# A hybrid decoder layer on one core: the input scales of all token tiles worked out beside the first pair's

## The chip, the cores and the metric

The kernel runs on one core of one Trainium2 chip. The metric is the device time of one execution in microseconds. The core has five engines with instruction queues of their own, each worked off in order: PE (matrix products and transposes), DVE (vector work), ACT (elementwise functions), POOL (here mainly indirect loads and additions) and SP (which issues transfers). They wait for each other by semaphores.

## The reference

One decoder layer over x of 1024 tokens by 1024 features, f32, depth 1:

```
h  = x
xn = rmsnorm(h, norm_mix)                       # x * rsqrt(mean(x*x) + 1e-6) * gain
z  = xn @ w_in ; q, k, v, a, gt = split(z)
attn = dilated causal attention(rope(q), rope(k), v), 8 heads of 64,
       patterns (128,1), (512,4), (2048,16) merged by their softmax denominators
c    = silu(layernorm(depthwise causal conv of 31 taps(a * sigmoid(gt)) + conv_b))
h += concat(rmsnorm(attn), rmsnorm(c)) @ w_out
xn = rmsnorm(h, norm_ffn)
s  = (xn @ peer_wq) against two tables of 128 sub-keys, 8 heads;
     top 16 of each half, top 16 of their sums -> 128 experts of 16384 per token, softmax gate
h += sum_k gelu(xn . expert_u[e_k]) * gate_k * expert_v[e_k]
h += sigmoid(rmsnorm(h, norm_ple) @ w_ple_gate) * (p @ w_ple_proj)
out = rmsnorm(h, final_norm)
```

The change concerns the first line's mean of squares of x alone.

## The kernel before, in words

The 1024 tokens are eight tiles of 128, taken in four pairs (GROUPS). A pair g goes through stages: stage_in (normed_input, then qkv), stage_attend (attend, then convolve), stage_out (mixed, project, normed_ffn), stage_search and stage_combine. They are written in the order in0, attend0, then for pair 0 out0, search0, in1, combine0, attend1, then in2, out1, search1, attend2, combine1, then in3, out2, search2, attend3, combine2, and last out3, search3, combine3. "Pair 1" below means tiles 2 and 3, the second pair.

normed_input is what the change splits. It takes the pair's two tiles xt (tag "xn", two buffers, loaded by SP), squares each on ACT with a running sum (sqj_mix, L146), takes the root on ACT (sd_mix, L151) and the reciprocal on DVE (r_mix, L153), scales xt by it on ACT (L286), transposes each xt in two batches of four through one PSUM bank (pt_mix, L162) and evicts each batch to xT with the gain (ACT, L167). PE's products for k, q, v (L261) and for the convolution's a and gt (L270) read xT.

Three PSUM banks with the tag "lin" serve k, q, v, a, gt, the output products, and the sums cs of the convolution as well. convolve works out 13 of the 31 taps as ACT products (tap, L349) that POOL adds into side (L350), with three tap buffers, and 18 taps as a chain on DVE in a lin bank (L353, L356); cc (L358) adds both and frees the bank. mixed transposes cc on PE (pc, L423) for the layer norm.

Retrieval is done in two ways. Tiles 2 to 5 (ALL) go through a dense product with every expert (dense): 128 steps of key columns, PE's longest part. Tiles 0, 1, 6, 7 (FEW) fetch their 128 rows of expert_u and of expert_v per token by indirect loads, 1024 transfers that POOL issues (L596), with one multiply-and-sum on DVE each (L609 for u, L625 for v) and a ring of six buffers. embed is the last stage: the dense tiles and tile 0 first, then tiles 1, 6 and 7.

The order of each engine's instructions is fixed when the kernel is built: a scheduler walks through the written program and, by its own estimate of when operands are ready, puts the ready instruction of the highest priority next. Stages that are written one behind the other so run interleaved, and the gathers, which have the lowest priority, fill what the scheduler holds to be gaps on DVE. On the chip the queues then run in that order, whatever is ready.

## Time and profile before

| | us |
|---|---|
| median of three runs | 3139.38 |
| the three runs | 3140.76, 3117.92, 3139.38 |
| profiled execution | 3130.95 |
| its span, from the first to the last instruction | 3129.1 |
| mean granted clock of TensorE, of full speed | 0.943 |
| first matmul of the dense product starts | 1412.15 |

Read the table with the sections of the program in mind: up to 1412 us come the four pairs and the making of the dense product's gates, then the dense product to about 2928, then the last embeds. Queries of the trace give busy time by stretch, the waits of an engine with what released it, and the single instructions in order of time. In these, "idle before" is the time in which the engine did nothing before the instruction, and the arrow names what came last of what it waited for.

### The profile page before, as it was taken

What the parts mean: (1) busy time and instruction counts of PE and PEld (TensorE: products, weight loads), DVE (VectorE), ACT (ScalarE), POOL (GpSimd) and SP (SyncE); (2) the same over time, 40 slices, a digit from 0 to 9 for tenths busy, and PEclk for the clock granted to TensorE, in tenths of its full rate; (3) what the DMA queues carried; (4) which work ended last, traced back from release to release, by engine and by line L of the source; (5) the groups of instructions that cost most, each with busy time, mean ns of one, the idle gap of its engine ahead of it and who ended that gap; (6) DMA issues with size and microseconds to landing.
All of it is one profiled execution on the core that took longest, in us unless ns stands there. A gap on an engine that the chain in (4) does not pass through costs nothing. (4 is left out here: it accounts for less than half of the span.)

```text
span 3129.1 us, 36005 instructions
## 1 busy us (share of the span) xinstructions
PE 2734.5 (87%) x11711; PEld 2003.1 (64%) x11711; DVE 2503.7 (80%) x5164; ACT 1133.9 (36%) x2084; POOL 1495.5 (48%) x1220
## 2 busy tenths in 40 slices
PE   6588948977995689968999999999999999999986
PEld 3465624853674376647777777777777777777643
DVE  1528877998797889977898888988888888888871
ACT  2523443274244329963222222222222222222342
POOL 0400676454436430134655655666655656655640
PEclk9799978988998799989999999999999999999998
DMA  4154859846854775799999999999999999998970
GB/s 166 54 175 140 311 203 361 302 149 233 319 202 161 266 272 154 231 297 333 346 351 331 340 326 352 350 350 351 339 331 332 347 340 344 339 334 321 332 261 24
DMA packets 304527, 865.75 MB, mean 277 GB/s; under 512 B 26779, under 2 KB 93747, under 8 KB 304339
## 3 DMA queue, kind: packets, MB, share of 16 engines
q0 software_dynamic: 147456, 536.94, 47.3%
q1 hardware_dynamic: 153616, 323.16, 29.8%
q10 hardware_dynamic: 3266, 3.36, 0.3%
q8 instruction: 92, 1.51, 0.2%
q14 instruction: 97, 0.79, 0.1%
HBM read 819.83 MB, written 43.52 MB: 276 GB/s over the span
## 5 line engine op out<-in xcount | busy, mean ns | idle before, releaser
L596 POOL DMA_INDIRECT u<-in_expert_u_dram,ex x512 | 675.9, 1320 | 822.3 <-DVE hk L609 547.1
L596 POOL DMA_INDIRECT v<-in_expert_v_dram,ex x512 | 671.5, 1312 | 510.7 <-DVE gy L625 376.9
L625 DVE SCALAR_TENSOR_TENSOR gy<-v,ga,gy 128x1024 f32<-128x1024 f32 x512 | 657.8, 1285 | 41.0 <-DMA v<-in_expert_v_dram,ex 31.9
L609 DVE CUSTOM_DVE_ANT_0 u<-u,gxn 128x1024 f32<-128x1024 f32 x512 | 613.7, 1226 | 54.5 <-DMA u<-in_expert_u_dram,ex 53.4
L741 PE MATMUL ph<-xh,uh 128*128 128x512 f32 x1024 | 407.4, 398 | 43.5 <-DMA gt<-gate_d 29.0
L743 PE MATMUL ph<-xh,ul 128*128 128x512 f32 x1024 | 409.5, 400 | 21.5 <-DVE ul L719 21.1
L759 ACT CAST vh<-v 128x1024 fp32r<-128x1024 f32 x128 | 131.5, 1051 | 757.1 <-PE kept_y L774 516.2
L742 PE MATMUL ph<-xl,uh 128*128 128x512 f32 x1024 | 404.9, 395 | 0.0
L741 PEld LDWEIGHTS ph<-xh,uh 128*128 128x128 f32 x1024 | 196.2, 192 | 91.2 <-ACT uh L717 49.0
L743 PEld LDWEIGHTS ph<-xh,ul 128*128 128x128 f32 x1024 | 195.4, 191 | 75.9 <-DVE ul L719 35.4
L761 DVE TENSOR_TENSOR vl<-v,vh 128x1024 fp32r<-128x1024 f32 x128 | 154.2, 1225 | 109.7 <-ACT vh L759 109.2
L350 POOL TENSOR_TENSOR side<-side,tap 128x256 f32<-128x256 f32 x192 | 147.8, 772 | 193.8 <-ACT tap L349 132.4
L772 PE MATMUL py<-vh,ah 128*128 128x512 f32 x512 | 204.8, 400 | 38.4 <-ACT ah L751 38.4
L270 PE MATMUL pq<-x2T,w_pq 128*128 128x256 f32 x1024 | 231.4, 384 | 4.8 <-DMA w_pq<-in_peer_wq_dram 3.4
L742 PEld LDWEIGHTS ph<-xl,uh 128*128 128x128 f32 x1024 | 196.2, 192 | 41.9
L270 PEld LDWEIGHTS pq<-x2T,w_pq 128*128 128x128 f32 x1024 | 194.2, 193 | 34.0 <-issue 3.4
L773 PE MATMUL py<-vl,ah 128*128 128x512 f32 x512 | 201.7, 397 | 0.0
L774 PE MATMUL kept_y<-vh,al 128*128 128x512 f32 x512 | 199.7, 390 | 0.0
L772 PE MATMUL kept_y<-vh,ah 128*128 128x512 f32 x512 | 199.5, 390 | 0.0
L774 PE MATMUL py<-vh,al 128*128 128x512 f32 x512 | 199.2, 397 | 0.3 <-DVE al L753 0.3
L773 PE MATMUL kept_y<-vl,ah 128*128 128x512 f32 x512 | 199.4, 389 | 0.0
L717 ACT CAST uh<-u 128x1024 fp32r<-128x1024 f32 x128 | 134.2, 1048 | 108.8 <-DMA u<-in_uT_dram 67.7
(264 smaller groups left out, 4683.0 us busy)
## 6 DMA issues: line engine op xcount, KB each, us to landing
u<-in_uT_dram SPq DMA_DIRECT2D x128, 512.0 KB, 6.9
v<-in_expert_v_dram SPq DMA_DIRECT2D x128, 512.0 KB, 6.3
w_pq<-in_peer_wq_dram SPq DMA_DIRECT2D x64, 512.0 KB, 5.0
gate_d<-stage SPq DMA_DIRECT2D x16, 2048.0 KB, 11.8
gt<-gate_d SPq DMA_DIRECT2D x64, 512.0 KB, 10.1
w_o<-in_w_out_dram SPq DMA_DIRECT2D x32, 512.0 KB, 4.8
w_k<-in_w_qkv_dram SPq DMA_DIRECT2D x16, 512.0 KB, 6.3
w_q<-in_w_qkv_dram SPq DMA_DIRECT2D x16, 512.0 KB, 4.4
```

Source lines behind the costliest of these rows:

```text
L270: nc.tensor.matmul(a, w[:, k, :], xT[:, k, :], start=k == 0, stop=k == KD - 1)
L350: G.tensor_tensor(side, side, m, ALU.add)
L596: d = G.indirect_dma_start(out=e, out_offset=None, in_=table, in_offset=bass.IndirectOffsetOnAxis(ap=index, axis=0))
L609: uses(V.tensor_tensor_reduce(out=e, in0=e, in1=xn, scale=1.0, scalar=0.0, op0=ALU.mult, op1=ALU.add, accum_out=hk[:, k : k + 1]))
L625: uses(V.scalar_tensor_tensor(y, e, act[:, k : k + 1], y, ALU.mult, ALU.add))
L741: nc.tensor.matmul(ph, hi, xh[:, k, :], start=k == 0, stop=False)
L742: nc.tensor.matmul(ph, hi, xl[:, k, :], start=False, stop=False)
L743: nc.tensor.matmul(ph, lo, xh[:, k, :], start=False, stop=k == KD - 1)
L761: V.tensor_tensor(b, v, a.bitcast(F32), ALU.subtract)
L772: nc.tensor.matmul(py, ah[e][:, rows(j)], vh[e][:, half(f)], start=first, stop=False)
L773: nc.tensor.matmul(py, ah[e][:, rows(j)], vl[e][:, half(f)], start=False, stop=False)
L774: nc.tensor.matmul(py, al[e][:, rows(j)], vh[e][:, half(f)], start=False, stop=last_e)
```

## The change

The mean of squares is taken out of normed_input. input_scales(g, xs) works out r for a pair and keeps its columns in r_mix; pair 0's is called just ahead of stage_in(0). later_scales, called behind stage_in(0), loads the six tiles of pairs 1 to 3 a second time (xq2 to xq7, tag "t4", two buffers, on SP's queue) and works out their scales. normed_input then only scales and transposes. The reciprocals get a tag of their own ("r_mix", four buffers).

```diff
--- before.py
+++ after.py
@@ -138,18 +138,18 @@
     acc = bank(ps_keep, "acc", 1)
 
 
-    def rstd(srcs, n, name, junk=None, pool=small):
+    def rstd(srcs, n, name, junk=None, pool=small, r_tag="r"):
 
         ssq = pool.tile([P, len(srcs)], F32, tag="ssq", name=f"ssq_{name}", bufs=2)
         for j, src in enumerate(srcs):
             sq = junk(f"sqj_{name}_{j}") if junk else mpool.tile([P, D], BF16, tag="t2", name=f"sqj_{name}_{j}", bufs=3)
             S.activation(sq[:, :n], src, AF.Square, accum_out=ssq[:, j : j + 1])
-        return inv_sqrt(ssq, 1.0 / n, name, pool)
-
-    def inv_sqrt(v, scale, name, pool=small):
+        return inv_sqrt(ssq, 1.0 / n, name, pool, r_tag)
+
+    def inv_sqrt(v, scale, name, pool=small, r_tag="r"):
         sd = pool.tile([P, v.shape[1]], F32, tag="sd", name=f"sd_{name}", bufs=2)
         S.activation(sd, v, AF.Sqrt, bias=eps, scale=scale)
-        r = pool.tile([P, v.shape[1]], F32, tag="r", name=f"r_{name}", bufs=4)
+        r = pool.tile([P, v.shape[1]], F32, tag=r_tag, name=f"r_{name}", bufs=4)
         V.reciprocal(r, sd)
         return r
 
@@ -279,11 +279,24 @@
             xs.append(xt)
         return xs
 
+    def input_scales(g, xs):
+        r = rstd(xs, D, f"mix{g}", r_tag="r_mix")
+        for j, i in enumerate(GROUPS[g]):
+            r_mix[i] = r[:, j : j + 1]
+
+    def later_scales():
+        for g in range(1, NG):
+            xs = []
+            for i in GROUPS[g]:
+                xt = mpool.tile([P, D], F32, tag="t4", name=f"xq{i}", bufs=2)
+                nc.sync.dma_start(xt, x_d[rows(i), :])
+                xs.append(xt)
+            input_scales(g, xs)
+
     def normed_input(g, xs):
-        r = rstd(xs, D, f"mix{g}")
         xT = apool.tile([P, KD, GN], F32, tag="xT", name=f"xT{g}")[:, :, : len(xs) * P]
         for j in range(len(xs)):
-            S.activation(xs[j], xs[j], AF.Copy, scale=r[:, j : j + 1])
+            S.activation(xs[j], xs[j], AF.Copy, scale=r_mix[GROUPS[g][j]])
             transpose_to(xT[:, :, rows(j)], xs[j], KD, f"mix{g}_{j}", tps, g_mix)
         return xT
 
@@ -826,7 +839,7 @@
     xs = load(0)
     load_tables()
     fetched, wide, h1s = {}, {}, {}
-    st = {}
+    st, r_mix = {}, {}
 
     def stage_in(g):
         xT = normed_input(g, xs if g == 0 else load(g))
@@ -854,7 +867,9 @@
             else:
                 wide[i] = combine(i, vals[j], idxs[j], mpool, ND)
 
+    input_scales(0, xs)
     stage_in(0)
+    later_scales()
     stage_attend(0)
     for g in range(NG - 1):
         if g > 0:
```

The kernel's lines behind the new function are 13 further down in the changed file, those of the last part 15.

The first place is the opening on ACT. sqj_mix is a Square with its sum, xt and xq are tiles of x, sd_mix a root, skT the copy of the transposed sub-keys:

```order
 L146 ACTIVATE sqj_mix_1_164,ssq_mix_161<-xt_105 128x1024
+L146 ACTIVATE sqj_mix_0_367,ssq_mix_366<-xq_362 128x1024
+L164 COPY skT<-pt_sk_157 128x256
 L151 ACT_TABLE_LOAD
 L151 ACTIVATE sd_mix_166<-ssq_mix_161,eps 128x2
-L164 COPY skT<-pt_sk_157 128x256
-L286 ACTIVATE xt_103<-xt_103,r_mix_168 128x1024
-L286 ACTIVATE xt_105<-xt_105,r_mix_168 128x1024
+L146 ACTIVATE sqj_mix_1_369,ssq_mix_366<-xq_364 128x1024
+L299 ACTIVATE xt_103<-xt_103,r_mix_168 128x1024
+L299 ACTIVATE xt_105<-xt_105,r_mix_168 128x1024
+L151 ACTIVATE sd_mix_371<-ssq_mix_366,eps 128x2
```

The root of pair 0 and the table load ahead of it have moved behind skT, and Squares and roots of the later pairs stand between them and the scaling of pair 0's tiles.

The second place is PE at the input of pair 2 (tiles 4 and 5), behind the last convolution product a_3. Before:

```order
L270 MATMUL a_3_2290<-xT_1545,w_a_3_2288 128x256 x8
L162 MATMUL pt_mix_0_0_2554<-cst,xt_2539 128x128 x4
L261 MATMUL k_0_2592<-w_k_0_2594,xT_2552 128x512
L162 MATMUL pt_mix_0_4_2563<-cst,xt_2539 128x128 x4
L261 MATMUL k_0_2592<-w_k_0_2594,xT_2552 128x512
L261 MATMUL k_0_2592<-w_k_1_2600,xT_2552 128x512
L162 MATMUL pt_mix_1_0_2573<-cst,xt_2541 128x128 x4
L261 MATMUL k_0_2592<-w_k_1_2600,xT_2552 128x512
L261 MATMUL k_1_2593<-w_k_0_2594,xT_2552 128x512
L162 MATMUL pt_mix_1_4_2582<-cst,xt_2541 128x128 x4
```

and with the change:

```order
L270 MATMUL a_3_2320<-xT_1575,w_a_3_2318 128x256 x8
L162 MATMUL pt_mix_0_0_2575<-cst,xt_2569 128x128 x4
L162 MATMUL pt_mix_0_4_2584<-cst,xt_2569 128x128 x4
L162 MATMUL pt_mix_1_0_2594<-cst,xt_2571 128x128 x4
L162 MATMUL pt_mix_1_4_2603<-cst,xt_2571 128x128 x4
L261 MATMUL k_0_2613<-w_k_0_2615,xT_2573 128x512 x2
L261 MATMUL k_0_2613<-w_k_1_2621,xT_2573 128x512 x2
L261 MATMUL k_0_2613<-w_k_2_2627,xT_2573 128x512 x2
L261 MATMUL k_1_2614<-w_k_0_2615,xT_2573 128x512 x2
L261 MATMUL k_1_2614<-w_k_1_2621,xT_2573 128x512 x2
```

The four batches of transposes used to alternate with matmuls of k; now all four stand directly behind a_3, and k's first six matmuls belong to the pair's first tile alone.

The third place is DVE where the dense product begins. ul is the first instruction of it, u_56 is the gather of tile 1's 57th row with its reduction, hk its result. Before:

```order
L609 ISA u_55_19701,hk_19533<-u_55_19701,gxn_19534 128x1024
L609 ISA hk_19533 128x1
L609 ISA u_56_19704,hk_19533<-u_56_19704,gxn_19534 128x1024
L609 ISA hk_19533 128x1
L719 TENSOR_TENSOR ul_9124<-u_9120,uh_9122 128x1024
L609 ISA u_57_19707,hk_19533<-u_57_19707,gxn_19534 128x1024
```

and with the change:

```order
L622 ISA u_35_19653,hk_19545<-u_35_19653,gxn_19546 128x1024
L622 ISA hk_19545 128x1
L622 ISA u_36_19656,hk_19545<-u_36_19656,gxn_19546 128x1024
L622 ISA hk_19545 128x1
L732 TENSOR_TENSOR ul_9136<-u_9132,uh_9134 128x1024
L622 ISA u_37_19659,hk_19545<-u_37_19659,gxn_19546 128x1024
```

Up to this place tile 1 has 57 of its u rows behind it before, and 37 with the change.

## Rows read from the trace of the kernel before

**Rows 1.** Page part 1: busy us (share of span), instructions of each engine.

```profile
PE 2734.5 (87%) x11711; PEld 2003.1 (64%) x11711; DVE 2503.7 (80%) x5164; ACT 1133.9 (36%) x2084; POOL 1495.5 (48%) x1220
```

**Rows 2.** Windows: length; PE, PEld, DVE, ACT, POOL busy; clock; DMA share; GB/s.

```profile
250.00:1412.00 1162.00, 944.57 (x4384) 634.60 (x4382) 986.68 (x2961) 563.25 (x1195) 506.39 (x463) 0.90 0.70 241
1412.00:2928.00 1516.00, 1441.12 (x6148) 1162.92 (x6149) 1326.38 (x1753) 406.92 (x525) 889.38 (x650) 0.98 0.93 339
```

**Rows 3.** Waits of PE, 250 to 1412 us: total, times, longest.

```profile
PE pt_mix L162 <- ACT xt L286: 80.7, 3, 39.3
PE pc L423 <- DVE cc L358: 30.7, 3, 13.8
```

**Rows 4.** Timeline, ACT, opening: start, us, engine, line, operation [idle before].

```profile
17.34 1.06 ACT L146 ACTIVATE sqj_mix<-xt 128x1024 bf16<-128x1024 f32 x1
...
19.54 1.28 ACT L151 ACT_TABLE_LOAD   x1
20.84 0.29 ACT L151 ACTIVATE sd_mix<-ssq_mix,eps 128x2 f32<-128x2 f32 x1
24.39 0.37 ACT L164 COPY skT<-pt_sk 128x256 f32<-128x256 f32 x1 [3.26 <-PE pt_sk L162]
```

**Rows 5.** Timeline, PE, opening: the long run of K.

```profile
34.97 9.61 PE L261 MATMUL k<-w_k,xT 128*128 128x512 f32 x22
```

**Rows 6.** Windows, opening, between the first loads and the next.

```profile
23.00:37.00 14.00, 11.34 (x33) 6.06 (x34) 0.00 (x0) 7.02 (x19) 0.00 (x0) 1.00 0.01 1
```

**Rows 7.** DMA issues of the first 60 us: count, KB, us to landing.

```profile
xt<-in_x_dram SPq DMA_DIRECT2D x2, 512.0 KB, 5.4
```

**Rows 8.** Timeline, pair 1: last score matmul, r_mix, first transposes.

```profile
263.78 0.94 PE L486 MATMUL psc<-skT,pqT 128*128 128x128 f32 x7
...
272.91 0.14 DVE L153 RECIPROCAL r_mix<-sd_mix 128x2 f32<-128x2 f32 x1
...
274.28 1.12 PE L162 MATMUL pt_mix<-cst,xt 128*128 128x128 f32 x4 [9.56 <-ACT xt L286]
```

**Rows 9.** Timeline, pair 2: convolution sums and r_mix on DVE; PE.

```profile
406.53 0.41 DVE L358 TENSOR_TENSOR cc<-cs,side 128x256 f32<-128x256 f32 x1
...
407.76 13.40 DVE L356 SCALAR_TENSOR_TENSOR cs<-glu,cw,cs 128x256 f32<-128x256 f32 x34
421.07 0.41 DVE L358 TENSOR_TENSOR cc<-cs,side 128x256 f32<-128x256 f32 x1
428.13 0.42 DVE L358 TENSOR_TENSOR cc<-cs,side 128x256 f32<-128x256 f32 x1 [6.64 <-POOL side L350]
428.47 0.16 DVE L153 RECIPROCAL r_mix<-sd_mix 128x2 f32<-128x2 f32 x1
...
429.87 1.12 PE L162 MATMUL pt_mix<-cst,xt 128*128 128x128 f32 x4 [39.27 <-ACT xt L286]
...
451.47 1.88 PE L261 MATMUL q<-w_q,xT 128*128 128x512 f32 x4
```

**Rows 10.** Windows, pair 2, behind the convolution.

```profile
440.00:460.00 20.00, 18.46 (x52) 8.53 (x51) 13.04 (x31) 3.38 (x8) 13.27 (x11) 1.00 0.99 385
```

**Rows 11.** Timeline, pair 3: DVE's wait for POOL, and PE.

```profile
713.15 0.42 DVE L358 TENSOR_TENSOR cc<-cs,side 128x256 f32<-128x256 f32 x1 [4.75 <-POOL side L350]
...
716.02 1.12 PE L162 MATMUL pt_mix<-cst,xt 128*128 128x128 f32 x4 [31.88 <-ACT xt L286]
```

**Rows 12.** Lines, DVE, 250 to 1412 us: one v gather's multiply-add.

```profile
L625 DVE SCALAR_TENSOR_TENSOR gy<-v,ga,gy 128x1024 f32<-128x1024 f32 x128 | 165.5, 1293 | 15.0 <-DMA v<-in_expert_v_dram,ex 13.2
```

**Rows 13.** Waits of ACT, 355 to 430 us; windows, attention of pair 1.

```profile
ACT tap L349 <- POOL side L350: 24.3, 44, 2.3
...
300.00:390.00 90.00, 87.82 (x393) 57.46 (x393) 74.03 (x159) 39.32 (x76) 58.21 (x48) 1.00 0.88 305
```

**Rows 14.** Timeline, DVE, tail: last gathers, last embed's start.

```profile
3024.08 5.24 DVE L625 SCALAR_TENSOR_TENSOR gy<-v,ga,gy 128x1024 f32<-128x1024 f32 x4
...
3097.22 0.16 DVE L153 RECIPROCAL r_ple<-sd_ple 128x1 f32<-128x1 f32 x1 [1.00 <-ACT sd_ple L151]
```

## The prediction

> **What bounds the kernel now.** I read the page's totals first: PE is busy for 87% of the span and DVE for 80% [rows 1]. A share over the whole span decides nothing, so next come the stretches [rows 2]. The middle one, the dense product, keeps PE busy for 1441.12 of 1516 us, and the change touches nothing in it. The first 1412 us hold the change. From 250 us to there PE is busy 944.57 of 1162 us. The waits of PE in that stretch say what holds it [rows 3]: 80.7 us in three waits of the input transposes pt_mix for the scaled tile xt, and 30.7 us of pc for the convolution sums cc. Those three waits are what the change aims at, one per later pair. Tracing each back is the next view. For pair 1, PE stands 9.56 us, and the scale 1/rms (r_mix) that xt needs is one row of DVE that runs at 272.91, behind the top-16 search [rows 8]. For pair 2, PE stands 39.27 us. On DVE r_mix is at 428.47, behind 34 convolution steps and a cc that itself waited 6.64 us for POOL [rows 9]. For pair 3 it is 31.88 us, behind a cc that waited 4.75 us [rows 11]. So in each of the three places a 0.16 us reciprocal waits in DVE's order, and PE with it.
>
> **The change, part by part.** Squares, roots, reciprocals, scales and transposes are as many as before, so their cost is a matter of place; new are six loads of 512 KB.
>
> *Opening.* Before, the table load (1.28 us) and the root ran while ACT anyway waited 3.26 us for pt_sk [rows 4]. Now skT's copy stands ahead of the table load, so the load is exposed, with one root (0.29) and the Square of xq3 (1.06 us [rows 4]) before the first xt scale: 1.28 + 0.29 + 1.06 = 2.6 us later. The other Squares stand between the four evictions of xT, where the first scale and eviction leave ACT time between transposes; I add 0.7 us, two thirds of one Square, for what doesn't fit. Sum **+3.3 us** on the long run of K, which began at 34.97 [rows 5]. Bounds: 1.28 + 0.29 = +1.6 if the Squares all fit, and 6 x 1.06 + 1.6 = +8 if none does. The loads themselves cost nothing in bandwidth: the DMA engines were 0.01 busy between 23 and 37 us [rows 6], the landing of such a load took 5.4 us [rows 7], and six times 0.5 MB fill that stretch. If the stretch were full, each would cost its share of the landing, inside the +8.
>
> The rule that speaks against this stands in the Trainium skill, DMA: Bandwidth & Descriptors, section "Anatomy of one DMA": a wait for a semaphore is taken on the issuing sequencer before the transfer is dispatched. By that rule w_k_3 stands on SP's queue behind xq6 and xq7, which wait for buffers that Squares on ACT free, and the opening would come to its upper bound, +8. No row of before has a load blocked in this way, so it shows neither for nor against.
>
> *Pair 1.* The transposes no longer wait for DVE. The last score matmul of the search ends at 264.72, that is 263.78 + 0.94, and pt_mix began at 274.28 [rows 8]: 8.9 us can go, after 0.66 us for the copy that frees its PSUM bank. But ACT now scales pair 2's first tile ahead of pair 1's last eviction, and that tile's load can start only when pair 1's first buffer is read; against the landing of 5.4 us [rows 7] I charge 2 us, since K's first matmuls need only the earlier evictions. **-7 us**, bounds -3 (all 5.4 us shown) and -9. What is late next is DVE, which is busy here.
>
> *Pair 2.* The four transposes now run directly behind a_3, in the gap. The 39.27 us don't go whole, since K still needs PSUM banks in which convolution sums lie: three "lin" banks serve both. K's first tile gets the bank that a cc at 406.53 frees, its second the one of the cc at 421.07 [rows 9]. From there eight matmuls of K on the second tile, and its last weights once a slot is free, take some 10 us: K ends at about 431 instead of 451.47, where q begins [rows 9], which is 20 us for PE. DVE and the gathers don't follow all of it. Behind the convolution come rotary steps and gathers at 1.29 us [rows 12], with the DMA engines at 0.99 from 440 to 460 [rows 10]; in the new order 26 gathers instead of 32 stand from the convolution to the layer norm, and six at 1.29 are 7.7 us; the 6.64 us wait for POOL goes as well, because the side taps start earlier. 7.7 + 6.6 = 14.3, and with the rotary steps no longer waiting for a late K **-15 us**. Bounds: -10 (K starts when the bank is free, at 421.5, and then takes as long as before from its first transpose on, 451.47 - 429.87 = 21.6 us: 443.1, or 8.4 sooner, and the first batch of transposes, 1.12 us, is no longer in it: about 10) and -20.
>
> *Pair 3.* The same with 31.88 us. The wait of 4.75 us for POOL goes and the transposes with their evictions are out of K's way; DVE is full with the combine step up to its layer norm, so I take **-12 us**, pair 2's in the ratio of the two gaps (31.88/39.27 x 15 = 12.2). Bounds -8 and -18.
>
> *Dense and tail.* The gathers fill DVE's idle time, and in the new order tile 1's u rows up to 36 stand ahead of the dense part instead of up to 56: 20 fewer, while the dense part holds as many as before. So about 19 come later, in the tail, at 1.31 us each (5.24 / 4 [rows 14]): 25 us of DVE. The last gather of before ends at 3029.3 (3024.08 + 5.24) and its tile's embed starts only at 3097.2 [rows 14]: 68 us of cover. They stand in DVE's order between the steps of the embeds, so I charge **+4 us**, bounds 0 and +8 (a third of the 25). Without that cover they would cost all 25.
>
> Sum: 3.3 - 7 - 15 - 12 + 4 = -26.7 us. Bounds together: 1.6 - 9 - 20 - 18 + 0 = -45 and 8 - 3 - 10 - 8 + 8 = -5. The profiled execution took 3130.95 us, so **3104 us**; that lies 35 us under the median of the three runs (3139.38), which is itself 8.4 above the profiled one.
>
> The table loads carry a second rule: the Trainium skill, ScalarE: Activation LUTs, section "What ACT_TABLE_LOAD costs", gives about 1.28 us for the load and as much again (1.38) for a drain. Here the root starts 1.30 us after its load [rows 4], so the trace shows no drain; by the skill the opening term would be +4.7.
>
> **The rivals.** A measurement of this kernel can tell about 1% from no change, some 31 us, so 3108 is the upper edge of "faster".
>
> *A, the forecast*: 3086 to 3115, chance 0.48, about two thirds of it under 3108.
>
> *B, given back*: PE is let go early, but the convolution and DVE's order hold the next step. For it: cc already holds PE for 30.7 us [rows 3], and in pair 2's gap DVE runs 34 convolution steps, 13.40 us, in one go [rows 9]. Against: 11.4 us of DVE's own waits for POOL (6.64 + 4.75) stand in the gaps. Terms at their small ends but the opening and tail as taken: 3.3 - 3 - 10 - 8 + 4 = -13.7, or 3117. Chance 0.22, and in it the case that the change does nothing since scales stay behind DVE, which the new order speaks against.
>
> *C, larger*: with the convolution begun earlier, the wait pc on cc goes too. For it: it has 30.7 us and follows the same stage. Half of it, 15, on top of the low bounds -9, -20, -18 with 3.3 + 0: 3130.95 - 59 = 3072. Chance 0.18; a part of it, with less of pc, lies above 3076.
>
> *D, slower*: ACT's order blocks. The scaled input lets the convolution of pair 1 start during its attention, so side taps on ACT now stand between exps, and each tap's buffer comes free by an add on POOL that stands behind a gather. There are 20 gathers between the adds of pair 1 now, 10 before, and 16 in pair 2. The longest such wait was 2.3 us and the sum around pair 1 24.3 us [rows 13], at a time when no exp stood behind. At 2.3 us, 20 of them are 46 us, and with pair 2's 83: 3130.95 - 27 + 46 = 3150, or 3187. Against: ACT is busy only 39.32 of 90 us and PE 87.82 in the stretch with attention [rows 13], so there are 51 us to swallow them. It decides once more than 27 us of the 83 show. Chance 0.12, half of it over 1%.
>
> **The numbers.** Faster by over 1%: two thirds of A and all of C, 0.32 + 0.18 = 0.50. Slower by over 1%: 0.06. Within: 0.16 + 0.22 + 0.06 = 0.44. The range that leaves out 2 in 10 goes from 3076 (leaves about 0.08, in C) to 3134 (leaves about 0.11, in D); A's own is 3086 to 3115.
>
> **What would show it.** The wait of pt_mix for xt should fall from 80.7 us to under 10; the long run of K should begin at about 38 us; pair 2's q should begin near 428 (451.47, less 20, less pair 1's 7, plus 3), the first dense matmul some 31 us earlier than now, and the dense stretch keep its 1516 us. The last gather should end 15 to 30 us nearer to the last embed. Wrong it would be if PE's gap after a_3 has a new releaser of the same length (B), if ACT's taps wait for POOL by far over 24 us with exps behind them (D), or if K's run begins at 42 us or later.

## The result, and the profile after

The changed kernel takes 3120.3 us (median of 20 runs, 3103.04 to 3128.67), the kernel before 3135.2 us beside it (20 runs, 3117.92 to 3144.91): a ratio of 0.995 [0.9936, 0.9963], or 15 us. It is faster by half a per cent: outside the interval of these runs, inside the 1% band that the prediction called no change. The forecast was 3104 us, 26.7 us under the profiled execution of before, so the time lies outside the forecast's own 3086 to 3115, inside its wide range of 3076 to 3134, and next to the 3117 of rival B. Profiled, the change has a span of 3119.6 us against 3129.1, only 9.5 us less, so the two profiles show two thirds of the gain that the medians show, and readings of single microseconds are to be taken with that in mind.

The page's totals of the changed kernel, as [rows 1]: no engine has more or less to do.

```profile
PE 2736.8 (88%) x11711; PEld 2003.7 (64%) x11711; DVE 2505.5 (80%) x5164; ACT 1129.3 (36%) x2083; POOL 1504.7 (48%) x1220
```

The windows of the changed kernel with the columns of [rows 2], cut at its own first dense matmul:

```profile
250.00:1390.00 1140.00, 957.36 (x4427) 645.87 (x4425) 968.26 (x2934) 552.29 (x1181) 492.96 (x443) 0.91 0.69 238
1390.00:2913.00 1523.00, 1437.56 (x6142) 1158.32 (x6143) 1325.00 (x1773) 405.26 (x524) 885.52 (x651) 0.99 0.93 337
```

The dense part begins at 1389.8 us instead of 1412.2, 22.3 us sooner, of which 9.5 are left at the end. From 250 us up to it PE's idle time fell from 217.4 us (1162.00 - 944.57) to 182.6 (1140.00 - 957.36). DVE's stayed as it was, 175.3 and 171.7 us, while its busy time fell by 18.4 us: of the 313 gathers that DVE worked off ahead of the dense part, 293 are left there. Going from mark to mark shows where. The marks are the start of K's long run, the first layer-norm statistics (bst) of pairs 1, 2 and 3 on DVE, the first dense matmul, the last one, and the end. All figures are us:

```
stretch                         before   change   difference   forecast
start to K's long run             35.0     42.5      +7.5        +3.3
K to pair 1's layer norm         451.9    430.8     -21.1       -7 - 15 = -22
pair 1's to pair 2's             285.9    272.6     -13.3       -12
pair 2's to pair 3's             244.9    256.1     +11.3         0
pair 3's to the first dense      394.5    387.8      -6.7         0
dense part                      1514.8   1523.1      +8.3         0
tail                             202.2    206.6      +4.4        +4
```

The waits that the change aimed at are gone. These are three of PE's waits in the changed kernel, 250 to 1412 us, as [rows 3]: what was waited for, the total, how often, the longest.

```profile
PE pc L436 <- DVE cc L371: 37.7, 3, 19.1
...
PE k L261 <- DVE cc L371: 19.5, 3, 7.0
PE pt_mix L162 <- ACT xT L167: 18.7, 6, 11.4
```

The 80.7 us of pt_mix for xt are no longer in the list. In their place stand 18.7 us of pt_mix for xT, the eviction that frees its PSUM bank, and 19.5 us of K for cc, where a PSUM bank still holds convolution sums; and pc's own wait grew from 30.7 to 37.7 us. Before, pt_mix and pc waited 80.7 + 30.7 = 111.4 us; now these three lines sum to 37.7 + 19.5 + 18.7 = 75.9, so 35.5 us of PE's waiting went.

**Pair 2** shows both replacements. Timeline of the changed kernel, PE with one row of ACT, and then DVE, as [rows 9]:

```profile
390.64 0.60 PE L162 MATMUL pt_mix<-cst,xt 128*128 128x128 f32 x4
...
401.43 1.12 ACT L167 ACTIVATE xT<-pt_mix,gains 128x128 f32<-128x128 f32 x4
...
402.60 1.12 PE L162 MATMUL pt_mix<-cst,xt 128*128 128x128 f32 x4 [11.36 <-ACT xT L167]
...
408.20 6.67 PE L261 MATMUL k<-w_k,xT 128*128 128x512 f32 x12
421.86 11.82 PE L261 MATMUL k<-w_k,xT 128*128 128x512 f32 x20 [6.99 <-DVE cc L371]
433.52 1.88 PE L261 MATMUL q<-w_q,xT 128*128 128x512 f32 x4
...
421.39 0.42 DVE L371 TENSOR_TENSOR cc<-cs,side 128x256 f32<-128x256 f32 x1
...
429.18 0.42 DVE L371 TENSOR_TENSOR cc<-cs,side 128x256 f32<-128x256 f32 x1 [6.42 <-POOL side L363]
```

The first transposes run at 390.64 behind a_3 as said, but the second batch waits 11.36 us, because the eviction of the first, at 401.43, stands in ACT's order behind side taps whose buffers POOL still holds. K's second half waits until the cc at 421.39 has read its bank. q begins at 433.52 instead of 451.47. DVE's wait for POOL, which the forecast let go, stayed (6.42 against 6.64 us).

**Pair 1** went as described. Timeline of the changed kernel, PE, as [rows 8]: the transposes stand directly behind the last score matmul, and the 9.56 us gap is 0.72.

```profile
271.21 1.16 PE L499 MATMUL psc<-skT,pqT 128*128 128x128 f32 x8 [0.68 <-ACT sc L501]
273.09 0.66 PE L162 MATMUL pt_mix<-cst,xt 128*128 128x128 f32 x4 [0.72 <-ACT sc L501]
```

**The opening** cost more than forecast. Timeline of the changed kernel, ACT and then PE, as [rows 4, 5]:

```profile
18.37 1.04 ACT L146 ACTIVATE sqj_mix<-xq 128x1024 bf16<-128x1024 f32 x1
...
28.30 0.37 ACT L164 COPY skT<-pt_sk 128x256 f32<-128x256 f32 x1 [8.80 <-PE pt_sk L162]
28.69 1.28 ACT L151 ACT_TABLE_LOAD   x1
29.99 0.29 ACT L151 ACTIVATE sd_mix<-ssq_mix,eps 128x2 f32<-128x2 f32 x1
30.19 1.04 ACT L146 ACTIVATE sqj_mix<-xq 128x1024 bf16<-128x1024 f32 x1
...
27.61 0.66 PE L162 MATMUL pt_sk<-cst,sk 128*128 128x128 f32 x2 [11.87 <-DMA sk<-in_sub_keys_dram]
...
42.51 1.88 PE L261 MATMUL k<-w_k,xT 128*128 128x512 f32 x4
```

The sub-keys, 23.70 us before, are used at 27.61, and behind them stand the table load, the root and a Square, as the working had it. K's long run begins with the row at 42.51. The DMA engines, idle in [rows 6] from 23 us on, are now busy there. Windows of the changed kernel (last two columns: DMA share and GB/s):

```profile
20.00:24.00 4.00, 0.00 (x0) 0.00 (x0) 0.00 (x0) 0.00 (x0) 0.00 (x0) 1.00 1.03 404
23.00:37.00 14.00, 3.84 (x9) 1.94 (x10) 0.33 (x2) 8.63 (x17) 0.00 (x0) 1.00 0.51 186
```

Just where the sub-keys are due, the DMA engines are full. That alone doesn't show why the sub-keys are late: before, the engines were as full from 16 to 20 us (1.01, 388 GB/s) with four 512 KB loads of h, and in the second profile of the change, below, they are full from 20 to 24 us (1.02, 375 GB/s) with the sub-keys used at 24.30.

**The last pair** gave 7 us back, where nothing was forecast. Timeline of the changed kernel: a row each of PE and POOL, ACT, DVE, then PE.

```profile
955.61 3.62 PE L270 MATMUL gt<-xT,w_gt 128*128 128x256 f32 x16
954.52 9.52 POOL L363 TENSOR_TENSOR side<-side,tap 128x256 f32<-128x256 f32 x7
...
956.34 0.51 ACT L362 ACTIVATE tap<-glu,cw 128x256 f32<-128x256 f32 x1 [1.82 <-POOL side L363]
...
965.92 0.51 ACT L362 ACTIVATE tap<-glu,cw 128x256 f32<-128x256 f32 x1 [1.34 <-POOL side L363]
966.34 0.36 ACT L344 ACTIVATE sg<-gt 128x256 f32<-128x256 f32 x1
...
966.74 0.55 DVE L366 TENSOR_SCALAR cs<-glu,cw 128x256 f32<-128x256 f32 x1 [4.43 <-ACT sg L344]
...
981.81 0.66 PE L436 MATMUL pc<-cst,cc 128*128 128x128 f32 x2 [19.13 <-DVE cc L371]
```

The same place in the kernel before, PE:

```profile
996.86 0.66 PE L423 MATMUL pc<-cst,cc 128*128 128x128 f32 x2 [12.08 <-DVE cc L358]
```

The sigmoid sg, a 0.36 us operation, stands on ACT behind eight taps that each wait for an add on POOL (956.34 to 965.92), though its input gt is there at 959.23 (955.61 + 3.62). It is not gathers that hold those adds: the twelve adds of this group of channels have 4 gathers among them on POOL, 8 before. Seven adds in a row take 9.52 us, up to 1.78 us each where most adds of this kernel take 0.73. DVE's convolution starts 4.43 us late for the sigmoid, and PE's wait is 19.13 us where it was 12.08.

**Tail**, DVE, as [rows 14]: 19 more gathers lie behind the last dense matmul; the last one starts at 3052.68 and still ends 33 us ahead of the last embed's r_ple, where 68 us lay before. So the two are 34.5 us nearer, over the 15 to 30 that were forecast.

```profile
3052.68 1.28 DVE L638 SCALAR_TENSOR_TENSOR gy<-v,ga,gy 128x1024 f32<-128x1024 f32 x1
...
3087.36 0.16 DVE L153 RECIPROCAL r_ple<-sd_ple 128x1 f32<-128x1 f32 x1 [1.01 <-ACT sd_ple L151]
```

### The profile page after: what moved, and what is told of

It reads as the page before. It is cut to its first block, busy times and chain, and to the rows that moved or that the text cites. A ratio compares the mean times of both kernels' runs of the same rounds, so it can differ in the third digit from the quotient of the medians.

```text
span 3119.6 us, 36029 instructions
## 1 busy us (share of the span) xinstructions
PE 2736.8 (88%) x11711; PEld 2003.7 (64%) x11711; DVE 2505.5 (80%) x5164; ACT 1129.3 (36%) x2083; POOL 1504.7 (48%) x1220
## 4 chain that ended last, share of the span: by engine, by line
PE 32%; DVE 20%; issue 17%; DMA 14%; POOL 11%; ACT 5%; POOLq 0%; ACTq 0%; DVEq 0%; SPq 0%
POOL v L609 5%; DMA v<-in_expert_v_dram 5%; PE pG L698 4%; DVE gy L638 3%; POOL u L609 3%; POOL side L363 3%; DVE u L622 3%; DMA v<-in_expert_v_dram,ex 3%; DMA u<-in_expert_u_dram,ex 2%; PE plg L819 2%; PE pq L270 2%; PE s L389 2%; PE py L785 2%; DVE cs L369 2%; PE py L787 1%
## 5 line engine op out<-in xcount | busy, mean ns | idle before, releaser
L363 POOL TENSOR_TENSOR side<-side,tap 128x256 f32<-128x256 f32 x192 | 155.4, 810 | 214.0 <-ACT tap L362 147.5
```

What stands on the lines that cost most here:

```text
L363: G.tensor_tensor(side, side, m, ALU.add)
```

## The experiments

All ratios are against the kernel before on the same chip, with a 95% interval.

**The price alone.** The kernel before, with the early scales also computed but not used: each later pair still works out its own.

```
     stage_in(0)
+    later_scales()        # results unused, tag r_mix
     stage_attend(0)
```

> The kernel before with the six extra loads of x, their Squares, roots and reciprocals behind the first pair's input stage, but with nobody using them: each pair still works out its scale itself, as before. Theory T (the price of the change is paid in the opening: the sub-keys' load lands 3.9 us later because the extra loads share the DMA engines, and the table load, a root and Squares are exposed on ACT for another 3.6 us, and the delay passes through to the end): the long run of K begins at 42 to 43 us instead of 34.97, and the time is 6 to 9 us above before, some 3142 where before is 3135. Rival R (the first 250 us have slack behind them, so an opening delay is swallowed by later waits): K late by the same, the time within 3 us of before.

Ratio 1.0018 [0.9999, 1.0037]: about 5 us of cost by the medians, at the edge of what the runs can tell from none. Timeline, PE:

```profile
24.36 0.66 PE L162 MATMUL pt_sk<-cst,sk 128*128 128x128 f32 x2 [8.00 <-DMA sk<-in_sub_keys_dram]
...
39.51 9.61 PE L261 MATMUL k<-w_k,xT 128*128 128x512 f32 x22
```

K is 4.5 us late with the sub-keys only 0.7 us late, the first dense matmul 8.0 us. The waits of pt_mix for xt stayed at 81.8 us, so the loads and Squares alone bring nothing.

**The price moved away.** The change, with the early scales worked out behind pair 0's attention.

```
     stage_in(0)
-    later_scales()
     stage_attend(0)
+    later_scales()
```

> The changed kernel with the call that works out the later scales moved from behind the first pair's input stage to behind its attention and convolution; all else the same. Theory T: the opening is as in the kernel before (K's long run at 35 us, the sub-keys landing at 23.7), the three later waits stay as short as with the change, and the time is 6 to 9 us under the change: 3112 where the change has 3120 and before 3135. Rival R: the opening is won back but swallowed later, time 3118 to 3122. Second rival: the moved Squares, with a root's table load of their own between attention's exps, cost a few us there, and half the gain goes.

Ratio 0.9936 [0.9913, 0.9959]. Timeline, PE:

```profile
23.54 0.66 PE L162 MATMUL pt_sk<-cst,sk 128*128 128x128 f32 x2 [7.34 <-DMA sk<-in_sub_keys_dram]
...
35.13 9.61 PE L261 MATMUL k<-w_k,xT 128*128 128x512 f32 x22
```

The opening is back at its time before (34.97), so its cost comes from where the early scales stand. Pair 1's layer norm comes 6.7 us sooner than in the change (466.6 against 473.3), but at the first dense matmul 0.6 us of that are left (1389.2): pair 2's stage took 279.3 us instead of 272.6, at a granted clock of 0.91 instead of 0.93. The ratio's interval covers the change's.

**The sub-keys first.** The change, with the sub-keys' load and transposes at the head of the tables' loads instead of their end.

```
+        sk = mpool.tile(...); nc.scalar.dma_start(sk..., sub_keys)
+        transpose_to(skT, sk, 2, "sk", pps)
         gr = mpool.tile(...)
...
         nc.scalar.dma_start(g_ffn, ...)
-        sk = ...; dma_start(sk ...); transpose_to(skT, sk, ...)
```

> The changed kernel with the sub-keys' load and transposition put first among the table loads on ACT's queue, so that it no longer stands behind the bias, the gains and the extra loads; the extra loads and Squares stay in the opening. Theory T splits the 7.5 us of the opening in 3.9 for the sub-keys' landing and 3.6 for ACT's own work: with the copy of the sub-keys out of the way before the Squares, K's long run begins at 36 to 38 us instead of 42.5, and the time is 4 to 6 us under the change. Rival: the Squares themselves wait for the landing of the extra loads (6.8 us each pair), so K begins at 40 or later and the gain is under 2 us.

Ratio 0.9929 [0.9909, 0.995]. pt_sk runs at 3.94 us, K's long run begins at 35.73, the first dense matmul at 1375.6. Timeline, PE:

```profile
35.73 9.61 PE L261 MATMUL k<-w_k,xT 128*128 128x512 f32 x22
```

With the sub-keys out of the way of x, and the table load free to run early, K begins 6.8 us sooner than in this profile of the change, and 4.4 sooner than in the second.

**Sums out of PSUM.** The change, with the convolution's running sums in an SBUF tile, so that K never waits for a bank that holds them.

```
-            sums = lin(f"cs{g}_{c}")[:, :gn]
+            sums = cc = apool.tile([P, GN], F32, tag="cc", ..., bufs=4)[:, :gn]
...
-            cc = apool.tile([P, GN], F32, tag="cc", ..., bufs=4)[:, :gn]
```

> The changed kernel with the convolution's sums kept in the SBUF tile that cc uses anyway, so that they no longer take the three PSUM banks that k, q and v need. Theory P (what is left of the gaps of pairs 2 and 3 is K waiting for a PSUM bank that a convolution sum holds: 19.5 us in three waits in the changed kernel): the waits of K for cc vanish, q of pair 2 begins 8 to 12 us earlier than with the change (433.5), that of pair 3 likewise, and the time is 10 to 15 us under the change. Rival D (DVE's convolution with the gathers behind it sets the pace; K would only stand and wait for its rotary steps): the wait of K moves to pt_k or to the rotary steps on DVE, the layer norms of pair 1 and 2 (473.3 and 745.9) move by under 4 us, and the time is within 5 us of the change.

Ratio 0.9958 [0.9939, 0.9978]: nothing won over the change. PE's waits, 250 to 1372 us, and then the timeline of DVE at the end:

```profile
PE k L261 <- ACT xT L167: 41.5, 4, 16.2
PE pc L435 <- DVE cc L370: 29.2, 3, 13.7
...
3096.55 3.96 DVE L637 SCALAR_TENSOR_TENSOR gy<-v,ga,gy 128x1024 f32<-128x1024 f32 x3 [0.90 <-DMA v<-in_expert_v_dram,ex]
3102.05 0.16 DVE L153 RECIPROCAL r_ple<-sd_ple 128x1 f32<-128x1 f32 x1 [1.54 <-ACT sd_ple L151]
```

K's wait for cc is gone, and a longer one for the evictions of xT took its place; still the dense part begins at 1372.6, 17.3 us sooner than in the change. The end comes no sooner. With less time ahead of the dense part, DVE did fewer gathers there, 261 instead of 293, 112 instead of 80 were left behind the last dense matmul, the last one ends at 3100.5, 1.5 us ahead of the last embed, and the tail took 230.4 us instead of 206.6. Here the tail's cover is used up, and time won early is paid back there.

**The sub-keys first, without the change.** The kernel before with the third experiment's edit.

```
+        sk = ...; dma_start(sk ...); transpose_to(skT, sk, ...)    # in front of gr, as above
```

> The kernel before with the sub-keys' load and transposition put first among the table loads on ACT's queue; nothing of the change in it. Theory T (opening time passes through): the wait of 3.26 us for the sub-keys goes, K's long run begins at 31 to 32 us instead of 34.97, and the time is about 3 us under before, which three rounds can hardly tell from zero. It gives what the change is worth once the sub-keys are out of the way: the third experiment less this one. On the dense stretch, which took 1515 and 1518 us without the change and 1524 to 1533 with it: if its length follows from the change, it is 1513 to 1519 here; if it only scatters from one execution to the next, anything from 1513 to 1533.

Ratio 0.9977 [0.9956, 0.9997]; K at 33.56, the first dense matmul at 1400.5. A part of the third experiment's gain over the change is thus not the change's.

**Sub-keys first and scales late.** The edits of the second and third experiments together.

```
+        sk = ... (in front of gr)
...
     stage_attend(0)
+    later_scales()
```

> The changed kernel with both: the sub-keys' load first, and the later scales worked out behind the first pair's attention and convolution. Theory T: nothing of the change is left in the opening, K's long run begins at 31 to 32 us (11 us earlier than with the change), and the time is 9 to 11 us under the change, ratio to before about 0.9915. Rival (what is won in the opening is swallowed before the dense product, as it was when only the later scales were moved: layer norm of pair 1 6.7 us earlier, that of pair 2 not): ratio 0.9935 to 0.995. The dense stretch takes 1524 to 1533 us if its length follows from the change.

Ratio 0.9921 [0.9897, 0.9945], median 3113.78 us; K at 32.07, the first dense matmul at 1381.3. It beats the kernel before, and by its middle value the change.

**Pair 1 alone.** The change, with early scales for pair 1 only; pairs 2 and 3 work out theirs as before.

```
-        for g in range(1, NG):
+        for g in (1,):
...
     def normed_input(g, xs):
+        if g > 1:
+            input_scales(g, xs)
```

> The changed kernel, but only pair 1's scale is worked out early; pairs 2 and 3 work out theirs in place, as before. Theory T: the opening still costs, since two extra loads stand ahead of the sub-keys and a root's table load and a Square are exposed: K's long run begins at 39 to 41 us, 4 to 6 late. Pair 1's transposes no longer wait (9.56 us), so its K run comes 3 to 5 us earlier than before; the gaps of 39 and 32 us in pairs 2 and 3 are there as before, and the time is within 6 us of before. Rival: the first gap is the one that counts, and the time falls by 10 or more.

Ratio 1.0001 [0.9986, 1.0016]. The wait for xt in pair 1 is gone, two remain (PE's waits, 250 to 1412 us):

```profile
PE pt_mix L162 <- ACT xt L301: 69.0, 2, 35.8
PE pc L438 <- DVE cc L373: 30.7, 3, 13.8
```

From K to pair 1's layer norm it took 11.9 us less than before (440.0 against 451.9), so pair 1's stage did what was forecast and more; but the opening cost 4.2 us and the stage of pair 3, which this edit doesn't touch, 12.5 us more, 12.0 of them as PE's busy time (212.9 us instead of 200.9). pc's wait is as long as before, so it is not the sigmoid here. The windows of this kernel (PE busy, PEld, DVE, ACT, POOL, granted clock, DMA share, GB/s) show what it is:

```profile
907.00:917.00 10.00, 8.89 (x51) 6.26 (x51) 10.00 (x62) 7.79 (x18) 8.64 (x11) 0.98 0.07 13
917.00:927.00 10.00, 10.00 (x25) 5.11 (x24) 6.26 (x51) 2.74 (x6) 1.90 (x3) 0.50 0.12 43
927.00:937.00 10.00, 10.00 (x31) 6.77 (x30) 4.77 (x10) 5.46 (x8) 2.05 (x2) 0.50 0.16 52
```

The kernel before, the same work:

```profile
923.00:933.00 10.00, 10.00 (x55) 6.75 (x55) 9.62 (x66) 6.18 (x14) 2.51 (x4) 1.00 0.32 99
```

In the attention of pair 3 the granted clock fell to 0.50, the lower level of 1.2 GHz, for some 20 us, with PE busy throughout, 8.89 of 10 us just before the fall; PE did 25 and 31 matmuls in 10 us where the kernel before did 55. Before, this stretch had the full 2.4 GHz.

**Pairs 2 and 3 alone.**

```
-        for g in range(1, NG):
+        for g in range(2, NG):
...
+        if g == 1:
+            input_scales(g, xs)
```

> The changed kernel, but only the scales of pairs 2 and 3 are worked out early; pair 1 works out its own in place. Theory T: the opening costs 6 to 8 us, pair 1's wait of 9.6 us is back, and pairs 2 and 3 gain 12 to 14 us each, as with the whole change: the dense product begins 12 to 16 us before 1412, and the time is 3 to 10 us under before. Rival (gains of pairs 2 and 3 need pair 1's, because its scale on ACT is what lets their tiles be scaled in time): the gap of pair 2 stays over 25 us and the time is at or over before.

Ratio 1.0008 [0.999, 1.0025]. PE's waits, 250 to 1402 us:

```profile
PE pt_mix L162 <- ACT xT L167: 23.7, 6, 17.1
PE k L261 <- DVE cc L373: 17.6, 3, 6.3
PE pt_k L162 <- DVE k L315: 12.1, 5, 6.9
PE pt_mix L162 <- ACT xt L301: 9.6, 1, 9.6
```

Its two big waits for xt are gone, yet from K to pair 1's layer norm it won 4.4 us, and from there to pair 2's 8.2, with waits for k (12.1 us of pt_k for the rotary steps) that the whole change has only in part (8.6). The first dense matmul came 10.1 us sooner, with 301 gathers ahead of it (313 before), and the dense part took 6.0 more. Neither half shows a gain by itself and the whole shows 15 us: the pairs' terms do not simply add.

**The sigmoid freed.** The sixth experiment's kernel, with the last pair's later taps ordered behind the sigmoid.

```
-            S.activation(sg, pg, AF.Sigmoid)
+            sig = S.activation(sg, pg, AF.Sigmoid)
...
-                    S.activation(m, xk, AF.Copy, scale=wk)
+                    tp = S.activation(m, xk, AF.Copy, scale=wk)
+                    if g == NG - 1 and c == 1 and k > 4:
+                        order_after(tp.ins, sig.ins.name)
```

> The sixth experiment's kernel (sub-keys first, later scales behind the first pair's attention) with one thing more: in the last pair, the side taps of the second channel group from its sixth on are ordered behind the fourth gate's sigmoid on ACT. Theory S (rival D of the prediction, in the last pair: that sigmoid stands behind eight taps that wait for POOL, the convolution's first sums on DVE start 4.4 us and more late, and PE's wait of pc for cc is 19.1 us instead of 12.1 in every run with the whole change, 37.7 against 30.7 us in all): DVE's wait of cs for sg goes, PE's waits of pc for cc are back at about 31 us, the stretch between the layer norms of pairs 2 and 3 is 5 to 8 us shorter, and the ratio to before falls from 0.992 to about 0.990. Rival: the taps that are held back make cc wait for POOL's side instead (now 4.9 us there), and nothing is won. The dense stretch takes 1519 to 1533 us if its length follows from the change, 1512 to 1522 if not.

Ratio 0.9918 [0.9895, 0.9942]. Timeline, ACT and PE:

```profile
953.31 0.38 ACT L344 ACTIVATE sg<-gt 128x256 f32<-128x256 f32 x1 [5.53 <-PE gt L270]
...
970.18 0.66 PE L438 MATMUL pc<-cst,cc 128*128 128x128 f32 x2 [13.45 <-DVE cc L373]
```

The sigmoid waits for its own input alone, DVE's wait for it is gone, pc's first wait is 13.45 us instead of the sixth experiment's 19.15, and the stage from pair 2's to pair 3's layer norm 253.0 us instead of 257.4. The total cannot be told from the sixth experiment's.

**A late start.** The kernel before, with 30 spare Squares ahead of the first root; nothing is left out.

```
+        if g == 0:
+            spare = ...
+            for n in range(30):
+                sq = ...
+                S.activation(sq, xs[0], AF.Square, accum_out=spare)
```

> The kernel before with 30 spare Squares of the first tile on ACT ahead of the first root, their sums unused: a delay of the opening by some 32 us, with the rest of the order as before. Theory T (the opening passes through one for one): K's long run begins at about 67 us instead of 35, and the time is 28 to 36 us above before, ratio 1.009 to 1.0115. Theory G (what the change takes off before the dense product comes back in part because the dense stretch is longer the earlier it begins; over the eleven profiles so far it is 1512 us where the dense product begins at 1420 and 1519 to 1533 where it begins at 1372 to 1390, about a third of a us back for each us): the dense stretch is 1503 to 1510 us here, the time only 18 to 24 us above before. Rival N (its length scatters and has nothing to do with when it begins): 1512 to 1525.

Ratio 1.0102 [1.008, 1.0124], 33 us by the medians (3173.62 against 3140.46). Timeline, PE:

```profile
71.97 8.32 PE L261 MATMUL k<-w_k,xT 128*128 128x512 f32 x19
```

K is 37.0 us late and, by the medians, the end 33: an opening microsecond is an end microsecond, nearly. The profiled execution is the slowest of the four (3185.73 us), and in it the end is 54.9 us late, 13.9 of them in the two stages from pair 1's to pair 3's layer norm, so its stages say less than the medians. The dense part, started at 1463.7, took 1518.0 us, so here its length does not follow from when it starts.

**The change again.** The changed kernel, unedited.

```
(no edit)
```

> The changed kernel once more, nothing edited, for a second profile of it on the chip that runs the delay. Its K run begins at 42 to 43 us, the waits of pc for cc sum to 37.7 us, the dense product begins at 1383 to 1396 us; the dense stretch tells how far two executions of one program differ: 1519 to 1533 if what was seen so far is the kernel's, anything from 1512 if it scatters. Ratio 0.995.

Ratio 0.9948 [0.9928, 0.9968]. Timeline, PE:

```profile
24.30 0.66 PE L162 MATMUL pt_sk<-cst,sk 128*128 128x128 f32 x2 [7.89 <-DMA sk<-in_sub_keys_dram]
...
40.09 9.61 PE L261 MATMUL k<-w_k,xT 128*128 128x512 f32 x22
```

The sub-keys are 3.3 us sooner than in the first profile of the same kernel, K 2.4 us. The stages repeat within 1 us (430.1, 272.1 and 256.5 us), the last pair's +11 and the dense part's 1522.4 too. So two executions agree on the stages; the sub-keys' landing is what scatters between them.

## Why the prediction was right, and where it was not

The sign was right, PE's waits for xt went as described, and the stage gains came out near their terms; the gain is about half of what was said (15 us by medians, 9.5 by profiles, of 26.7). The time itself is nearer to rival B's 3117 than to the forecast's 3104, but not for B's reason: the gains stand up to pair 2's layer norm, and what was lost was lost in places that the forecast had put at nothing or too low. Against the profiled sum, the missing 17 us are: opening +4.2, last pair +11.3, dense +8.3, tail +0.4, less 0.4 in pairs 1 and 2's stages and 6.7 behind pair 3.

**Opening, +3.3 forecast, +7.5 and +5.1 measured.** The term was mis-sized. From pt_sk to K's long run the change needs 14.9 us (15.8 in the second profile) against 11.3 before: that is the ACT part, +3.6 to +4.5, a little over the +3.3; the 0.7 us for Squares that don't fit were too few. The rest, 0.6 to 3.9, is pt_sk coming late. The prediction put the loads at no cost in bandwidth from the empty stretch between 23 and 37 us [rows 6], while the first early loads are issued at 12.88 us, beside the sub-keys' small load on another queue. But that the loads are what makes the sub-keys late is not shown: without early loads pt_sk came at 23.54, 23.70 and 24.20 us, with all six of them at 23.50 (fourth experiment), 24.30, 24.36 and 27.61, with some at 24.10 and 24.69. One execution in six stands out. Moving the sub-keys ahead, or the early scales behind, brings K back to within 0.8 us of before. That shows that place is the cost, to within the scatter of K's start: the sixth and the ninth experiment, which have the same opening, differ by 2.6 us (32.07 and 34.72). The prediction's own mark for being wrong here, 42 us or later, was met in one profile (42.51) and not in the other (40.09).

SP's load of w_k_3 was issued at 43.57 us instead of 36.02, but not because of the xq loads, the last of which went out at 36.70. It follows K's long run by 1.05 us before and by 1.06 in the change, and waits for PE's matmuls of K, as it did before (SP's waits, kernel before, 0 to 60 us):

```profile
SPq L249 <- PE k L261: 27.5, 4, 20.2
```

So a load blocked on its queue was there before, which the prediction overlooked, and the +8 that it set beside its sum did not come by that way; PE has no wait for w_k in the opening. These waits on SP's queue agree with the rule of the Trainium skill, DMA: Bandwidth & Descriptors, "Anatomy of one DMA", that a wait is taken on the issuing sequencer. The second rule weighed there, the Trainium skill's drain of about 1.38 us beside a table load (ScalarE: Activation LUTs, "What ACT_TABLE_LOAD costs"), is not seen here: the root starts 1.30 us after its table load again (28.69 to 29.99), with no drain in between.

**Pairs 1 and 2, -22 forecast, -21.1 measured; pair 3's transposes, -12 and -13.3.** The steps hold as a sum, for partly other reasons, and that the sum comes out so near is in part luck: 6.6 of pair 2's 15 us were to come from a wait for POOL that stayed. The PE side is as described: the gap behind a_3 is used, and K waits for cc's banks. DVE's wait for POOL did not go in pair 2's place (6.42 for 6.64 us) and went only in part in pair 3's (3.02 for 4.75). And the half experiments show that the split into terms was too neat: pair 1 alone wins 11.9 us up to its layer norm, pairs 2 and 3 alone 4.4 there and 8.2 behind.

A rival stands untested. The 20 gathers that left the stretch ahead of the dense part are, at 1.29 us each [rows 12], 25.8 us of DVE's time, more than the 22.3 us by which the dense part begins sooner, and DVE's idle time there hardly changed. From K's long run to the first dense matmul the profiles with 20 gathers fewer take 23 to 37 us less than before, the eighth experiment with 12 fewer 13.9 less, the fourth with 52 fewer 43.9 less, and the seventh with one fewer 3.3 more; those with none fewer scatter from 10.2 less to 14.5 more. How much of the stage gains is PE let go early, and how much is DVE's work moved under the tail's cover, no run separates: none held the gathers in their places.

**The last pair, 0 forecast, +11.3 measured.** This step was missing. Rival D's price did not come: ACT's taps waited 45.8 us for POOL between 250 and 1412 us, 46.5 before. But its mechanism, work on ACT held behind taps that wait for POOL, is there at one place: what stood behind the taps was not an exp but a sigmoid that DVE's convolution waits for, and POOL was slow by its adds and not by gathers. pc's wait has 7.0 of the 11.3 us, and the ninth experiment took 5.7 of pc's wait away by ordering alone, so that cause is shown. Why the adds are slow is not. Another 3.2 us are PE's busy time in that stage, 204.1 against 200.9 for the same matmuls, at a granted clock of 0.90 instead of 0.91. Where the half-clock stretches fall differs from profile to profile: over the profiles this stage has a clock between 0.88 and 0.93, and took 238.2 us at 0.93 and 257.4 at 0.88. That is read from rows; nothing was tried that held the clock, so it stays a reading. Rival C, by which pc's wait would shrink, was wrong: it grew.

**Behind pair 3, 0 forecast, -6.7 measured.** The 20 gathers fewer ahead of the dense part were counted against the tail, and not for this stretch, which has 80 of them where it had 86: an estimate of 7.7 us at 1.29 each. No run tested it alone.

**Dense part, 0 forecast, +8.3 measured.** Its cause is open. It has the same matmuls, and PE's busy time is no longer (1437.6 against 1441.1 us): by that profile it is idle time. In the second profile of the change the dense part is as long, but with PE idle about as before and busy 7 us longer, at a granted clock of 0.980 instead of 0.985. Six profiles without the whole change took 1511.5 to 1521.0 us, seven with it 1518.8 to 1532.2. The two sets overlap at the edge, and their means, 1517.8 and 1526.1, are 8 us apart, so that the change lengthens it is likely. It is not the start time alone (tenth experiment).

**Tail, +4 forecast, +4.4 measured.** Right, by its own reason: 19 gathers went there, under 68 us of cover. Over all profiles the tail goes with the gathers left in it: with 60 to 62 of them it is 2 us or less from before, with 79 or 80 it is 4.2 to 7.2 longer. The fourth experiment shows the other half of the prediction's reason: with another 32 gathers the cover is gone, and 24 us with it.

**A better version.** The sixth and the ninth experiments' kernels (0.9921 and 0.9918) beat the kernel before by 0.8%. Against the change (0.9936 to 0.9963) their intervals overlap at the edge, so that they beat it too is likely and not settled.

## What to carry to other kernels

Small work taken out of the middle must go to a place that is empty by the rows of the changed order: here the same work cost 5 us and more of the start in one place and nothing of it in another, behind the first pair's attention. When an in-order engine gets more waits behind a slow partner, look for every short operation queued there that another engine needs, not only for the ones in the loop you are changing. And where optional work, here the gathers, fills gaps and its rest lands at the end, measure that cover before counting time won early as time won.

## What the hardware showed unexpectedly

One small load, the sub-keys', was used at 24.3 us in one execution of the changed kernel and at 27.6 in another, with the DMA engines full from 20 to 24 us in both (375 and 404 GB/s), and at 23.5 with the same early loads in the fourth experiment (368 GB/s): a landing beside full engines is not one number.

Adds on POOL that mostly take 0.73 us took up to 1.78 in the last pair, and DVE's rows beside them were long too: one gather's multiply-add 1.74 us and the row of ge 1.74, where the ninth experiment, with its adds later, has 1.27 and 1.21. The two engines seem to slow each other there; no run tested it.

The granted clock can halve in the middle of a stage in which PE is busy, 20 us in the seventh experiment's kernel: a stage of the same work took 12.5 us more. It does not take an edit: in the second profile of the unedited change the clock is 0.50 from 881 to 890 us, with PE busy throughout, where the first has 1.00 in the same work (884.7 to 893.7). Stage times that differ by a few us must be compared together with their clock.
